# Every fourth weight rest made by ScalarE and an accumulating DMA in a float32 encoder trunk

## The chip, the core and the metric

The kernel runs on one core of a Trainium2 chip. The metric is the device time of one execution in microseconds (us); a kernel's time is the median of several runs. The five engines of a core (TensorE or PE, VectorE or DVE, ScalarE or ACT, GpSimd or POOL, SyncE or SP) run their own instruction queues in order and wait for each other by semaphores. DMAs are issued from such a queue (here from SP, POOL and twice from ACT) and are carried out by 16 DMA engines.

## The reference

A trunk of two layers on x of 256 tokens by 2048 features, float32. Per layer:

```
h = rms_norm(x);  z = h @ w_in                       # 2048 -> 11264 columns
ya = diff_attention(...); yb = dilated_mixture(...); yc = pool_mixer(...)
merged = g0 * (ya @ w_proj_a) + g1 * (yb @ w_proj_b) + g2 * (yc @ w_proj_c)
x = x + merged @ w_out
u = relu(rms_norm(x) @ w_up);  x = x + (u * u) @ w_down     # 2048 -> 8192 -> 2048
```

and a last rms_norm. Nearly all of the work is matmuls of the 256 tokens with weights that are read from HBM once.

## The kernel before, in words

To hold float32 accuracy at the rate of the type fp32r, each operand is split into a main part hi (the value rounded to fp32r) and a rest lo (value minus hi), and a product is three matmuls: hi with hi, hi with lo, lo with hi. `split` does that for activations, `convert` for weights.

The weights come in **steps** of 256 rows by 512 columns (512 KB). `add_unit` (L138) lists them; a unit is one block of 512 output columns, which is eight steps of a 2048-row weight (two or three of the projections' weights). There are 992 steps: per layer 80 for the inputs of the branches, 96 for the gates with 32 of the projections between them, 32 for w_out and 256 for the MLP, where four quarters of four w_up units are each followed by four w_down units.

`run_steps` (L180) goes through the steps. In step i it issues, in four slots, the step's matmuls, and in slot 2 (L201 to L203) the conversion of step i+3 and the load of the step four after the last one converted:

```
if slot == CONVERT_SLOT:
    convert(min(i + AHEAD, 2 * i + 1))
    fetch(st["cv"] - 1 + RAW_BUFS)
```

`fetch` (L143) loads a step into a tile raw by a DMA on SP's queue (L147); there are RAW_BUFS = 4 raw buffers. `convert` (L151) makes whi on ScalarE (L157) and wlo on VectorE (L158); there are AHEAD + 1 = 4 buffers of each. Buffers go around in order, so step j uses buffer j mod 4, and a buffer is free when its last reader is done: of raw the subtraction of wlo, of whi and wlo the matmuls. `by_token` (L162; activation stationary, 12 matmuls of 512 columns per step) is used by all units but w_up's, which go by `by_feature` (L172; weights stationary, 8 matmuls of 512 and 8 of 256 columns). After the last step of a unit its `after` function empties PSUM: `after_up` (L591) with ScalarE copies (u, L600), VectorE additions and squares (L601, L603) and, in the next two steps, splits into U (L242, L243); `after_down` (L613) with VectorE additions into x alone.

Other work is cut into pieces by generators, `side_work` (L115), and slipped between the slots: transposes, the attention (`attn_a`, `attn_b`), the pooling. On POOL's queue stand their loads of bias tables (`load_bias`, L364: biasa of 128 KB, biasb of 384 KB), the loads of the pooling bands (L488), the last norm's weight final_g (L631), the additions into merged (L538) and the small powers of the norms.

The order on each engine is the order in which this program issues; nothing reorders it later.

Of the kernel before, what the change touches and what calls it, by code (L numbers as in the profile page):

```python
# [10 lines left out]
F32 = mybir.dt.float32  # L11
FR = mybir.dt.float32r
BF16 = mybir.dt.bfloat16
ACTF = mybir.ActivationFunctionType
ALU = mybir.AluOpType
# [21 lines left out]
AHEAD = 3  # L37
CONVERT_SLOT = 2
RAW_BUFS = 4


def shape_constants():
    """Arrays that depend on the shapes alone: identity, T5 buckets of all
    distances, the windows of the dilated groups, the pooling bands."""
    ident = np.eye(128, dtype=np.float32)
    rel = (S - 1) - np.arange(512)
    half, exact = REL_BUCKETS // 2, REL_BUCKETS // 4
    n = np.abs(rel)
    nf = np.maximum(n, 1).astype(np.float32)
    ratio = (np.log(nf / np.float32(exact)) / np.float32(math.log(REL_MAX / exact))).astype(np.float32)  # L50
    large = exact + (ratio * np.float32(half - exact)).astype(np.int32)
    large = np.minimum(large, half - 1)
    bucket = np.where(rel > 0, half, 0) + np.where(n < exact, n, large)
    onehot = (np.arange(REL_BUCKETS)[:, None] == bucket[None, :]).astype(np.float32)
    window = np.zeros((REL_HEADS, 512), np.float32)
    for g, r in enumerate(DILATION):
        reach = (128, 512, 2048)[g] // (2 * r) * r
        ok = (rel % r == 0) & (n <= reach)
        window[A_HEADS + 4 * g:A_HEADS + 4 * g + 4, :] = np.where(ok, 0.0, NEG_INF)[None, :]
    pos = np.arange(S)  # L60
    band = np.zeros((S, len(C_WINDOWS), S), np.float32)
    for g, win in enumerate(C_WINDOWS):
        rad = win // 2
        lo, hi = np.clip(pos - rad, 0, S), np.clip(pos + rad + 1, 0, S)
        inside = (pos[:, None] >= lo[None, :]) & (pos[:, None] < hi[None, :])
        band[:, g, :] = inside / (hi - lo).astype(np.float32)[None, :] - np.eye(S)
    return {"c_ident": ident, "c_onehot": onehot, "c_window": window, "c_band": band.astype(np.float32)}
# [3 lines left out]
def encoder_trunk(ctx: ExitStack, tc: tile.TileContext, I, out: bass.AP):  # L71
    nc = tc.nc
# [28 lines left out]
    def tr_tile(shape, name):  # L101
        return ps_t.tile(shape, F32, tag="tr", name=name)

    # ---------------------------------------------------------------- side work
    lanes = []
    queue = []
    N_LANES = 2
# [5 lines left out]
        lanes.append([gen, False])  # L113

    def side_work():  # L115
        """The next piece of every side task, one at a time."""
        wait[0] -= 1
        if queue and busy[0] < N_LANES and wait[0] <= 0:
            lanes.append([queue.pop(0)(), True])
            busy[0] += 1  # L120
            wait[0] = SPACING
        for lane in list(lanes):
            yield lane
# [6 lines left out]
            if lane[1]:  # L130
                busy[0] -= 1

    # ---------------------------------------------------------------- weights
    steps = []
    st = {"dma": 0, "cv": 0}
    raw_t, hl_t = {}, {}
# [14 lines left out]
    def convert(upto):  # L151
        while st["cv"] <= min(upto, len(steps) - 1):
            j = st["cv"]
            r = raw_t.pop(j)
            hi = hl_p.tile([128, 2, BLK], FR, tag="hi", name="whi")
            lo = hl_p.tile([128, 2, BLK], FR, tag="lo", name="wlo")
            nc.scalar.activation(out=hi, in_=r, func=ACTF.Copy)  # L157
            nc.vector.tensor_tensor(out=lo, in0=r, in1=hi.bitcast(F32), op=ALU.subtract)  # L158
            hl_t[j] = (hi, lo)
            st["cv"] += 1  # L160

    def by_token(ps, a, kc, n, w, kk, t):  # L162
        """ps[token tile t] += act[kc].T @ W, the activation stationary."""
        hi, lo = w
        ts = slice(128 * t, 128 * t + 128)
        first, last = kc == 0, kc == n - 1
        o = ps[t][:, 0, :] if isinstance(ps, list) else ps[:, t, :]
        nc.tensor.matmul(o, a[:, kc, 0, ts], hi[:, kk, :], start=first, stop=False)  # L168
        nc.tensor.matmul(o, a[:, kc, 0, ts], lo[:, kk, :], start=False, stop=False)  # L169
        nc.tensor.matmul(o, a[:, kc, 1, ts], hi[:, kk, :], start=False, stop=last)  # L170

    def by_feature(ps, a, kc, n, w, kk, j):  # L172
        """ps[j] = [main | rest] of W[:, feature tile j].T @ act[kc], the weights stationary."""
        hi, lo = w
        fs = slice(128 * j, 128 * j + 128)
        first, last = kc == 0, kc == n - 1
        nc.tensor.matmul(ps[j], hi[:, kk, fs], a[:, kc, :, :], start=first, stop=False)  # L177
        nc.tensor.matmul(ps[j][:, S:2 * S], lo[:, kk, fs], a[:, kc, 0, :], start=False, stop=last)  # L178
# [41 lines left out]
                    u["after"](ps)  # L220

    def feature_banks(u):
        """Four PSUM banks; every other unit borrows those of the attention and the transposes."""
        if L["c"]["up"] % 2 == 0:
            g = [ps_g.tile([128, 2, BLK], F32, tag="g", name="acc") for _ in range(2)]
            u["groups"] = [(g[0], 0, 2), (g[1], 2, 2)]
            banks = [g[0][:, 0, :], g[0][:, 1, :], g[1][:, 0, :], g[1][:, 1, :]]
        else:
            a = ps_s.tile([128, 2, BLK], F32, tag="sc", name="acc")
            b = [ps_t.tile([128, 1, BLK], F32, tag="tr", name="acc") for _ in range(2)]  # L230
            u["groups"] = [(a, 0, 2), (b[0], 2, 1), (b[1], 3, 1)]
            banks = [a[:, 0, :], a[:, 1, :], b[0][:, 0, :], b[1][:, 0, :]]
        L["c"]["up"] += 1
        L["groups"] = u["groups"]
        return banks

    # ---------------------------------------------------------------- pieces
    def split(dst, src, scale=None):
        """dst[:, 0] gets the leading bits of src (times scale), dst[:, 1] the rest."""
        hi, lo = dst  # L240
        if scale is None:
            nc.scalar.activation(out=hi, in_=src, func=ACTF.Copy)  # L242
# [4 lines left out]
                                           op0=ALU.mult, op1=ALU.subtract)  # L247

    class Norm:
        """Statistics of the rows of x, block by block, and x * g transposed."""  # L250

        def __init__(self, g):
            self.ss = sm_p.tile([128, 2, NB], F32, tag="ss", name="ss", bufs=2)
# [30 lines left out]
        nc.scalar.activation(out=junk, in_=src, func=ACTF.Square, accum_out=dst)  # L284

    def rsqrt_mean(ss, n, name, w=2):
        """(mean + eps) ** -0.5 from partial sums of squares."""
        ms = sm_p.tile([128, w], F32, tag="ms", name="ms")
        rs = sm_p.tile([128, w], F32, tag=name, name=name, bufs=3)
        nc.vector.tensor_reduce(out=ms, in_=ss, axis=AX.X, op=ALU.add)  # L290
# [6 lines left out]

    L = {}

    # ---------------------------------------------------------------- q, k, v  # L300
    def qkv_tile():
        c = L["c"]
        if "Q" not in c:
# [173 lines left out]
            split((yT[:, h, 0, ts], yT[:, h, 1, ts]), tr, gsub[:, l:l + 1])  # L477
        return gen

    # ---------------------------------------------------------------- pooling  # L480
    def after_c(ps):
        c = L["c"]
        l = c["l"]
# [29 lines left out]
                yield  # L513
        start(task())

    # ---------------------------------------------------------------- gates
    def after_gate(ps):
        c = L["c"]
        g = one.tile([128, 2, BLK], F32, tag="gate", name="gate")
# [36 lines left out]
                start(task())  # L556
        return f

    # ---------------------------------------------------------------- residual
    def add_x(ps, n, scale=None, tiles=(0, 1)):  # L560
        cols = slice(n * BLK, (n + 1) * BLK)
        for t in tiles:
# [96 lines left out]
        c["rs8"] = sm_p.tile([128, 2], F32, tag="rs8", name="rs8", bufs=2)  # L659
        nc.vector.tensor_scalar(out=c["rs8"], in0=c["norm"].rs, scalar1=HD ** -0.5, scalar2=None, op0=ALU.mult)  # L660

    # ---------------------------------------------------------------- set-up
    def setup_norm1():
        tr = tr_tile([128, 16 * DEPTH], "v1t")
        nc.tensor.transpose(tr, vin1, ident[0:16 * DEPTH, 0:16 * DEPTH])
# [62 lines left out]
        nc.tensor.matmul(tr, ones, dl, start=True, stop=True)  # L728
        nc.vector.tensor_copy(out=neglam, in_=tr)

    # ---------------------------------------------------------------- program
    def queue_attention(kind):
        def add():
            c = L["c"]
# [102 lines left out]
```

## Time and profile before

| | |
|---|---|
| median of 3 runs | 2905.48 us (2901.34 to 2905.69) |
| span of the profiled execution, first to last instruction | 2904.1 us |
| PE busy | 2884.4 us, 99% |
| VectorE busy | 1582.5 us, 54% |
| ScalarE busy | 1353.5 us, 47% |
| GpSimd busy | 110.2 us, 4% |
| mean granted TensorE clock | 0.998 |
| mean busy share of the DMA engines | 0.63, 186 GB/s |

The profile is one execution. Its own time is given by its span alone; it is 1.4 us under the median of the runs. DMA instructions on an engine's queue are not counted as busy time of that engine. A PE that is busy 99% issues matmuls nearly all the time; matmuls overlap, so their durations add up to more than the time they take (a matmul of 512 columns lasts 0.39 us, and the next starts sooner).

### The profile page before, as it was taken

Reading aid. Unit: us, or ns where it says so; the run is one execution under the profiler, and the core shown is the slowest. Engines: PE = TensorE matmul, PEld = TensorE weight load, DVE = VectorE, ACT = ScalarE, POOL = GpSimd, SP = SyncE. Lnnn points to the kernel's source line nnn. Section 1 sums busy time; section 2 is a strip of 40 time slices with the busy share of each in tenths; the row PEclk is TensorE's granted clock in tenths of the full one; section 3 lists DMA queues with packets and bytes.
Section 4 is the critical chain, followed back from the end, with each engine's and each line's share of the span. In section 5 each row is a group of like instructions: output and inputs, shape, how many; then the busy total and the mean of one; then the engine's idle time right before and its main releaser. Section 6 shows DMA issues by size and latency. Waiting matters only on the chain.

```text
span 2904.1 us, 35814 instructions
## 1 busy us (share of the span) xinstructions
PE 2884.4 (99%) x13942; PEld 2396.0 (83%) x13942; DVE 1582.5 (54%) x1901; ACT 1353.5 (47%) x1716; POOL 110.2 (4%) x128
## 2 busy tenths in 40 slices
PE   8999999999999999999999999999999999999998
PEld 7877888888888888888888778888888888888887
DVE  5456544555655655555544565445555555555564
ACT  5455545444543434444444554544444444344443
POOL 1000001000000000000000000011100000000001
PEclk9999999999999999999999999999999999999999
DMA  7656766665666666666576567666656566666664
GB/s 236 193 159 177 196 173 158 188 188 182 186 195 192 181 197 188 190 184 192 188 206 186 161 176 200 168 165 192 183 187 200 190 189 188 193 179 198 190 188 156
DMA packets 275994, 540.00 MB, mean 186 GB/s; under 512 B 17044, under 2 KB 17230, under 8 KB 275696
## 3 DMA queue, kind: packets, MB, share of 16 engines
q1 hardware_dynamic: 271344, 523.63, 59.4%
q0 software_dynamic: 4144, 13.28, 3.0%
q8 instruction: 109, 1.79, 0.2%
q10 hardware_dynamic: 336, 0.80, 0.1%
q14 instruction: 61, 0.50, 0.0%
HBM read 535.51 MB, written 2.13 MB: 185 GB/s over the span
## 4 chain that ended last, share of the span: by engine, by line
PE 97%; DMA 1%; DVE 1%; issue 0%; ACT 0%; POOL 0%; POOLq 0%; DVEq 0%; SPq 0%; ACTq 0%
PE acc L168 23%; PE acc L170 23%; PE acc L169 22%; PE acc L177 16%; PE acc L178 8%; PE scb L385 1%; PE ob L412 1%; DMA biasb<-bias_d 1%; PE sca L435 1%; DMA raw<-in_w_in_dram 0%; PE xt L274 0%; PE oa L462 0%; PE qkt L344 0%; PE etb L402 0%; DVE wlo L158 0%
## 5 line engine op out<-in xcount | busy, mean ns | idle before, releaser
L158 DVE TENSOR_TENSOR wlo<-raw,whi 128x1024 fp32r<-128x1024 f32 x992 | 1225.4, 1238 | 1045.6 <-ACT whi L157 1037.5
L157 ACT ACTIVATE whi<-raw 128x1024 fp32r<-128x1024 f32 x992 | 1045.9, 1057 | 1049.5 <-PE acc L170 673.0
L177 PE MATMUL acc<-H,whi 128*128 128x512 f32 x2048 | 723.9, 399 | 0.6
L178 PE MATMUL acc<-H,wlo 128*128 128x256 f32 x2048 | 574.2, 280 | 0.0
L168 PE MATMUL acc<-whi,H 128*128 128x512 f32 x1408 | 569.8, 405 | 0.0
L170 PE MATMUL acc<-whi,H 128*128 128x512 f32 x1408 | 551.0, 391 | 0.0
L169 PE MATMUL acc<-wlo,H 128*128 128x512 f32 x1408 | 550.0, 391 | 0.5 <-DVE wlo L158 0.5
L177 PEld LDWEIGHTS acc<-H,whi 128*128 128x128 f32 x2048 | 384.7, 188 | 97.8 <-DVE x L567 2.5
L168 PE MATMUL acc<-whi,U 128*128 128x512 f32 x1024 | 399.1, 390 | 0.0
L170 PE MATMUL acc<-whi,U 128*128 128x512 f32 x1024 | 398.5, 389 | 0.0
L169 PE MATMUL acc<-wlo,U 128*128 128x512 f32 x1024 | 398.4, 389 | 0.0
L178 PEld LDWEIGHTS acc<-H,wlo 128*128 128x128 f32 x2048 | 386.6, 189 | 0.3
L168 PEld LDWEIGHTS acc<-whi,H 128*128 128x128 f32 x1408 | 265.2, 188 | 63.1 <-issue 11.5
L170 PEld LDWEIGHTS acc<-whi,H 128*128 128x128 f32 x1408 | 264.9, 188 | 57.6
L169 PEld LDWEIGHTS acc<-wlo,H 128*128 128x128 f32 x1408 | 265.7, 189 | 52.2 <-DVE wlo L158 2.1
L170 PEld LDWEIGHTS acc<-whi,U 128*128 128x128 f32 x1024 | 192.2, 188 | 40.4
L168 PEld LDWEIGHTS acc<-whi,U 128*128 128x128 f32 x1024 | 192.2, 188 | 39.7
L169 PEld LDWEIGHTS acc<-wlo,U 128*128 128x128 f32 x1024 | 192.3, 188 | 39.5
L168 PE MATMUL acc<-whi,M 128*128 128x512 f32 x256 | 101.2, 395 | 0.0
L170 PE MATMUL acc<-whi,M 128*128 128x512 f32 x256 | 99.9, 390 | 0.0
L169 PE MATMUL acc<-wlo,M 128*128 128x512 f32 x256 | 99.6, 389 | 0.0
L538 POOL TENSOR_TENSOR merged<-merged,gp 128x512 f32<-128x512 f32 x32 | 50.5, 1598 | 575.8 <-DVE gp L537 575.8
(153 smaller groups left out, 1709.3 us busy)
## 6 DMA issues: line engine op xcount, KB each, us to landing
raw<-in_w_in_dram SPq DMA_DIRECT2D x352, 512.0 KB, 4.1
raw<-in_w_up_dram SPq DMA_DIRECT2D x256, 512.0 KB, 3.8
raw<-in_w_down_dram SPq DMA_DIRECT2D x256, 512.0 KB, 4.5
raw<-in_w_out_dram SPq DMA_DIRECT2D x64, 512.0 KB, 4.3
raw<-in_w_proj_a_dram SPq DMA_DIRECT2D x24, 512.0 KB, 7.5
raw<-in_w_proj_b_dram SPq DMA_DIRECT2D x24, 512.0 KB, 4.2
raw<-in_w_proj_c_dram SPq DMA_DIRECT2D x16, 512.0 KB, 4.6
biasb<-bias_d POOLq DMA_DIRECT2D x16, 384.0 KB, 9.4
```

The lines of the kernel that those rows point to most:

```text
L157: nc.scalar.activation(out=hi, in_=r, func=ACTF.Copy)
L158: nc.vector.tensor_tensor(out=lo, in0=r, in1=hi.bitcast(F32), op=ALU.subtract)
L168: nc.tensor.matmul(o, a[:, kc, 0, ts], hi[:, kk, :], start=first, stop=False)
L169: nc.tensor.matmul(o, a[:, kc, 0, ts], lo[:, kk, :], start=False, stop=False)
L170: nc.tensor.matmul(o, a[:, kc, 1, ts], hi[:, kk, :], start=False, stop=last)
L177: nc.tensor.matmul(ps[j], hi[:, kk, fs], a[:, kc, :, :], start=first, stop=False)
L178: nc.tensor.matmul(ps[j][:, S:2 * S], lo[:, kk, fs], a[:, kc, 0, :], start=False, stop=last)
L385: nc.tensor.matmul(sc[:, g, :], head_rows(c, "qb", 4 * g + j)[:, ts], head_rows(c, "kb", 4 * g + j), start=True, stop=True)
L412: nc.tensor.matmul(o[:, g, :], eT[:, 2 * g + kc, :], c["vb"][:, kc, col:col + 64], start=kc == 0, stop=kc == 1)
L435: nc.tensor.matmul(sc[:, 2 * i, :], c["qa"][r, h, ts], c["ka"][r, h, :], start=True, stop=True)
L538: nc.gpsimd.tensor_tensor(out=mg[:, t, cols], in0=mg[:, t, cols], in1=e, op=ALU.add)
```

## The change

In steps 3, 7, 11 and so on, a quarter of all, ScalarE writes the negated weights, rounded to fp32r, into wlo (that is minus whi), and a DMA issued from POOL's queue adds the raw weights to it. The VectorE subtraction of these steps is gone. Docstrings and comment lines go too, which moves line numbers by five: whi is L158 now, the negated copy L160, the accumulating DMA L161 and the subtraction of the other steps L163.

```diff
 AHEAD = 3
 CONVERT_SLOT = 2
 RAW_BUFS = 4
+BY_DMA = 4
...
             nc.scalar.activation(out=hi, in_=r, func=ACTF.Copy)
-            nc.vector.tensor_tensor(out=lo, in0=r, in1=hi.bitcast(F32), op=ALU.subtract)
+            if j % BY_DMA == BY_DMA - 1:
+                nc.scalar.activation(out=lo, in_=r, func=ACTF.Copy, scale=-1.0)
+                nc.gpsimd.dma_start(out=lo, in_=r, accum_op=ALU.add)
+            else:
+                nc.vector.tensor_tensor(out=lo, in0=r, in1=hi.bitcast(F32), op=ALU.subtract)
             hl_t[j] = (hi, lo)
```

On SP the loads stay in their order. Here the end of a w_up unit's loads and the first of w_down's are shown, before and then changed; in brackets are the semaphores a load waits for (DVE: VectorE's, DMAHW: of DMAs issued by SP, DMASW: of DMAs issued by POOL):

```order
L147 DMA raw<-in_w_up_dram 128x2x512 [waits DMAHW5_49,DVE_49]
L147 DMA raw<-in_w_up_dram 128x2x512 [waits DMAHW6_49,DVE_49]
L147 DMA raw<-in_w_up_dram 128x2x512 [waits DMAHW7_49,DVE_49]
L147 DMA raw<-in_w_up_dram 128x2x512 [waits DMAHW0_49,DVE_49]
L147 DMA raw<-in_w_up_dram 128x2x512 [waits DMAHW1_49,DVE_49]
L147 DMA raw<-in_w_down_dram 128x2x512 [waits DMAHW2_49,DVE_49]
```

```order
L148 DMA raw<-in_w_up_dram 128x2x512 [waits DMAHW6_49,DVE_49]
L148 DMA raw<-in_w_up_dram 128x2x512 [waits DMAHW5_49,DMASW2_49]
L148 DMA raw<-in_w_up_dram 128x2x512 [waits DMAHW7_49,DVE_49]
L148 DMA raw<-in_w_up_dram 128x2x512 [waits DMAHW0_49,DVE_49]
L148 DMA raw<-in_w_up_dram 128x2x512 [waits DMAHW2_49,DVE_49]
L148 DMA raw<-in_w_down_dram 128x2x512 [waits DMAHW1_49,DMASW3_49]
```

Every fourth load now waits for a DMA of POOL's queue in place of VectorE.

On ScalarE, at the border of two w_up units, the evacuations u and splits U of the unit that ended stand around the first whi of the next one; before, and then changed:

```order
L157 ACTIVATE whi<-raw 128x1024 [waits DMAHW0_49,DVE_49,PE_49]
L600 ACTIVATE u<-acc 128x512 [waits PE_49]
L600 ACTIVATE u<-acc 128x256 [waits PE_49] x2
L242 ACTIVATE U<-u 128x2x256 [waits DVE_49]
L157 ACTIVATE whi<-raw 128x1024 [waits DMAHW1_49,Activation_49]
L242 ACTIVATE U<-u 128x2x256 [waits DVE_49]
```

```order
L158 ACTIVATE whi<-raw 128x1024 [waits DMAHW0_49,DVE_49,PE_49]
L605 ACTIVATE u<-acc 128x512 [waits PE_49]
L605 ACTIVATE u<-acc 128x256 [waits PE_49] x2
L247 ACTIVATE U<-u 128x2x256 [waits DVE_49]
L158 ACTIVATE whi<-raw 128x1024 [waits DMAHW1_49,Activation_49]
L160 ACTIVATE wlo<-raw 128x1024 [waits DMASW0_49]
L247 ACTIVATE U<-u 128x2x256 [waits DVE_49]
```

The whi of position 3 of the next unit is a changed step's, and the negated copy follows it, ahead of the second split.

On POOL, in the stretch where the dilated attention loads its biases and the projections are added into merged; before, and then changed:

```order
L364 DMA biasb<-bias_d 128x3x256 [waits DMASW7_49]
L364 DMA biasb<-bias_d 128x3x256 [waits DMASW0_49]
L538 TENSOR_TENSOR merged<-merged,gp 128x512 [waits DVE_49] x2
L364 DMA biasb<-bias_d 128x3x256 [waits DMASW1_49]
L364 DMA biasb<-bias_d 128x3x256 [waits DMASW2_49]
```

```order
L369 DMA biasb<-bias_d 128x3x256 [waits DMASW0_49]
L161 DMA wlo<-raw 128x1024 [waits DMASW7_49,DMAHW5_49,PE_49,Activation_49]
L369 DMA biasb<-bias_d 128x3x256
L161 DMA wlo<-raw 128x1024 [waits DMASW1_49,DMAHW1_49,PE_49,Activation_49]
L543 TENSOR_TENSOR merged<-merged,gp 128x512 [waits DVE_49] x2
L369 DMA biasb<-bias_d 128x3x256 [waits DMASW0_49]
L161 DMA wlo<-raw 128x1024 [waits DMASW3_49,DMAHW5_49,PE_49,Activation_49]
```

The accumulating DMA, which waits for ScalarE's negated copy, stands between the bias loads and additions that were neighbours.

## Rows read from the trace of the kernel before

**Rows 1.** The page: busy time of TensorE, and the chain that ended last, by engine.

```profile
PE 2884.4 (99%) x13942; PEld 2396.0 (83%) x13942; DVE 1582.5 (54%) x1901; ACT 1353.5 (47%) x1716; POOL 110.2 (4%) x128
...
PE 97%; DMA 1%; DVE 1%; issue 0%; ACT 0%; POOL 0%; POOLq 0%; DVEq 0%; SPq 0%; ACTq 0%
```

**Rows 2.** Who waited for whom, TensorE alone: us in total, times, longest.

```profile
PE ob L412 <- DVE eTb L406: 2.3, 2, 1.3
PE acc L169 <- DVE wlo L158: 0.5, 2, 0.3
```

**Rows 3.** Timeline, end of a w_up unit: start, us, instruction, [idle before <-releaser].

```profile
828.05 1.06 ACT L157 ACTIVATE whi<-raw 128x1024 fp32r<-128x1024 f32 x1 [1.71 <-PE acc L177]
830.82 1.06 ACT L157 ACTIVATE whi<-raw 128x1024 fp32r<-128x1024 f32 x1 [1.71 <-PE acc L177]
832.33 0.60 ACT L600 ACTIVATE u<-acc 128x512 f32<-128x512 f32 x1 [0.44 <-PE acc L178]
...
835.73 1.05 ACT L157 ACTIVATE whi<-raw 128x1024 fp32r<-128x1024 f32 x1
...
836.80 1.22 DVE L158 TENSOR_TENSOR wlo<-raw,whi 128x1024 fp32r<-128x1024 f32 x1 [0.26 <-ACT whi L157]
```

**Rows 4.** Timeline, ScalarE, in the w_down unit after it.

```profile
844.62 1.06 ACT L157 ACTIVATE whi<-raw 128x1024 fp32r<-128x1024 f32 x1 [1.61 <-PE acc L170]
847.34 1.06 ACT L157 ACTIVATE whi<-raw 128x1024 fp32r<-128x1024 f32 x1 [1.66 <-PE acc L170]
```

**Rows 5.** Stretches, whi alone: its length, busy us (count), clock, DMA share, GB/s.

```profile
65.00:639.30 574.30, 195.28 (x187) 1.00 0.64 180
639.30:743.40 104.10, 38.77 (x37) 1.00 0.59 186
743.40:1457.40 714.00, 270.44 (x256) 1.00 0.62 189
```

**Rows 6.** The page's costliest groups: wlo and whi (busy, mean ns, idle before).

```profile
L158 DVE TENSOR_TENSOR wlo<-raw,whi 128x1024 fp32r<-128x1024 f32 x992 | 1225.4, 1238 | 1045.6 <-ACT whi L157 1037.5
L157 ACT ACTIVATE whi<-raw 128x1024 fp32r<-128x1024 f32 x992 | 1045.9, 1057 | 1049.5 <-PE acc L170 673.0
```

**Rows 7.** Who waited for whom, SP's queue: us in total, times, longest.

```profile
SPq L147 <- DVE wlo L158: 2107.9, 906, 6.4
```

**Rows 8.** DMAs to landing: issues (median us), and lines L147 and L488.

```profile
raw<-in_w_up_dram SPq DMA_DIRECT2D x256, 512.0 KB, 3.8
raw<-in_w_down_dram SPq DMA_DIRECT2D x256, 512.0 KB, 4.5
...
biasb<-bias_d POOLq DMA_DIRECT2D x16, 384.0 KB, 9.4
biasa<-bias_d POOLq DMA_DIRECT2D x24, 128.0 KB, 3.5
...
final_g<-in_final_g_dram POOLq DMA_DIRECT2D x1, 1024.0 KB, 5.2
...
DMA to landing us min/median/max: 3.4/4.3/15.2
...
DMA to landing us min/median/max: 6.8/8.7/10.5
```

**Rows 9.** The page's DMA queues: packets, MB, share of 16 engines.

```profile
q1 hardware_dynamic: 271344, 523.63, 59.4%
q0 software_dynamic: 4144, 13.28, 3.0%
```

**Rows 10.** Timeline of TensorE near 425 us, and the stretch after the gap.

```profile
425.28 0.72 PE L412 MATMUL ob<-qkv,eTb 128*128 128x64 f32 x4 [1.28 <-DVE eTb L406]
...
426.33 0.63 PE L169 MATMUL acc<-wlo,H 128*128 128x512 f32 x1
426.75 0.63 PE L170 MATMUL acc<-whi,H 128*128 128x512 f32 x1
...
425.70:429.10 3.40, 3.40 (x11) 2.72 (x10) 1.95 (x3) 1.68 (x4) 0.06 (x1) 0.51 0.82 193
```

## The prediction

> **What bounds the kernel now.** I read the engine shares and the chain of waits first: TensorE is busy 99% of the span and its matmuls are 97% of the chain that ended last [rows 1]. The list of who waited for whom, cut to TensorE, then shows how little is lost to anything the change could relieve: 2.3 us behind a VectorE copy in the attention and 0.5 us behind wlo, in the whole run [rows 2]. VectorE, which the change relieves, is not on the path. What matters is therefore whether the new way of making lo is ready in time.
>
> For that I read the beat. Where matmuls run alone, ScalarE's whi instructions start 2.77 us apart in an up unit and 2.72 us apart in a down unit [rows 3, 4]; each waits for TensorE to give back a buffer. So four weight steps, one turn of the change, last 11.1 us (up) or 10.9 us (down). The two matmul sub-layers together have 2 x 256 steps; one of them takes 714.0 us [rows 5], so one up unit of eight steps has 22.2 us and one down unit 21.8 us. The 32 steps of w_out take 104.1 us, 13.0 us per four. In the stretch ahead of it 187 steps take 574.3 us, 12.3 us per four, because attention and transposes are mixed in, unevenly [rows 5].
>
> **Parts that cost or give next to nothing.** 248 VectorE subtractions of 1.238 us go [rows 6]: 307 us off an engine that is busy 54%. Even if every wait of rows 2 went with them, that is 2.8 us, 0.1% of the time. 248 more ScalarE instructions come, of the shape, types and function of whi, so 1.057 us each [rows 6]: 262 us more, 47% becomes 56% of the span; they run in ScalarE's idle time before the next buffer (1.7 us in each plain step [rows 3]). If that cover were gone, each would delay the next whi by its 1.06 us, and a whi is made some three steps before its use.
>
> **The part that counts: a longer ring.** RAW_BUFS is 4, and so is the turn of the change, so the changed steps always use the same raw buffer. SP can load step j+4 into it only when nobody reads step j there. Today the reader is done with the subtraction, and SP's loads wait for it 906 times [rows 7]. Changed, SP waits for the accumulating DMA to land, and the next three loads stand behind that wait. So a turn can't be shorter than this chain: raw load to landing, whi, the negated copy, the accumulating DMA from issue to landing, and around again.
>
> Terms: the load 3.8 us, the median of w_up (all loads: least 3.4, median 4.3) [rows 8]; I take the low median because SP has just been held back, so that little is in flight beside the first load. Two ScalarE instructions, 2.1 us [rows 6]. Handoffs 0.15 us: the whi of 835.73 ends at 836.78, and VectorE, which waits for it, starts at 836.80 [rows 3]; I count four such, with some reserve for the two DMAs among them. That is 6.05 us without the accumulation.
>
> The accumulation itself, 512 KB within SBUF, reads two operands and writes one. No row shows such a DMA. From below: 128 KB through POOL's queue land in 3.5 us (biasa). From above: 384 KB in small rows in 9.4 us (biasb) [rows 8]. Nearest by the bytes read, two times 512 KB, are the 1 MB loads on POOL's queue: final_g in 5.2 us, the pooling bands in 6.8 and, in the crowded start, 10.5 us [rows 8]. I take 5.6 us, nearer to final_g, which like the accumulation is issued alone in the middle of the run. The turn is then 6.05 + 5.6 = 11.65, say 11.7 us; the ends are 9.6 us (3.5) and 15.5 us (9.4).
>
> That two operands are read weighs most in this choice. The Trainium skill says the same of reductions in a DMA (Collectives: The Full Stack, section on the bandwidth ceiling): the add costs nothing, but two sources have to be read, and the rate is halved. No run here shows that yet; by it 1 MB is the size to price, as the sum already does, and a price per byte written would give about the raw load's 3.8 us instead.
>
> Against the beat: in a down unit two turns take 23.4 instead of 21.8 us, +1.6 us, 32 times: 51 us. In an up unit something is added: the changed step at position 3 is converted while step 0 runs, and whi stands on ScalarE behind the evacuations (u) and the first split (U) of the unit before. There whi starts at 835.73, 4.91 us after the one before instead of 2.77 [rows 3]. Of that I add 2.3 us to the ring, because a raw load that lands 3.8 us after the turn begins would wait from there to about 6.1 us (2.7 us of the last step, then 3.4 us from 832.33 to 835.73). So an up unit takes 2 x 11.7 + 2.3 = 25.7 instead of 22.2 us, 32 times 3.5: 112 us. w_out, 13.0 us per turn, hides it. In the other 104 turns (992 steps without 512 and 64, over four) the mean of 12.3 is above 11.7, but the plain half of them is at 10.9: 52 x 0.8 = 42 us. There POOL's in-order queue also holds the accumulation behind biasb loads and the merged additions; 10 us for that. Sum: 51 + 112 + 42 + 10 = 215 us.
>
> The sum stands against the profiled span, 2904.1 us; the median of the runs is 1.4 us more, and I add that: 2905.5 + 215 = 3120 us. Two executions of this kernel agree within some 0.2% (2901 to 2906), so that I count as no change.
>
> The DMA engines can carry it: 248 x 0.524 MB are 130 MB. The load queue takes 59.4% for 523.63 MB, POOL's queue 3.0% for 13.28 MB [rows 9]: 15% more at the first rate, 29% at the second, on 63%. At the upper end transfers would queue, which is one more reason for a wide range upwards.
>
> **Rivals.**
>
> Hidden (the other side). If the accumulation lands like one raw load of its size, 3.8 us [rows 8], the turn is 9.9 us: below 10.9, and in an up unit 2 x 9.9 + 2.3 = 22.1 against 22.2. Everything is covered, 2906 us. It decides at 3.9 us for up units and at 4.8 us for down units. For it: the DMA engines are free 37% of the time, and the whole add happens in SBUF. Against it: 128 KB already take 3.5 us on this queue, and no 1 MB load lands under 5.2 us [rows 8]. The Trainium skill's fit for a DMA that GpSimd issues (DMA: Bandwidth & Descriptors, section on the anatomy of one DMA) is 2.0 us plus the bytes at 436 GB/s; as an estimate that is 3.2 us for 512 KB and 4.4 us for 1 MB, and by 3.2 us the change would be hidden, at 2906 us, and by 4.4 us up units alone would lose 1.0 us each, 2937 us. The trace disagrees upwards: 5.2 us or more for 1 MB.
>
> Slow accumulation. If the read, add and write-back go at the pace of biasb, 9.4 us, the turn is 15.5 us: up 32 x 11.1, down 32 x 9.2, w_out 16 x 2.5, the others 104 x 3.2, together 1022 us, 3930 us. At 7.5 us the turn is 13.6: 234 + 173 + 10 + 135 = 552, 3458 us. For it: POOL's queue took long for 384 KB; against it: those were 1 KB rows from HBM, these are 4 KB rows in SBUF.
>
> The clock falls. At 425.28 TensorE had been idle for 1.28 us; in the 3.4 us that follow the granted clock is 0.51, the 1.2 GHz level, and matmuls start 0.42 us apart instead of 2.72/12 = 0.23 [rows 4, 10]. That costs about 1.6 us (8 matmuls in 3.4 us, which else take 1.8). The stalls forecast here are of that size. If each of 248 turns lost 1.6 us, 397 us more, 3517 us; where the ring is the bound TensorE has that time to spare, so I take half, 3320 us.
>
> Faster: only by rows 2, 0.1%, or by effects on the loads that nothing here shows.
>
> **How the numbers follow.** Forecast (accumulation between 4.2 and 7.5 us) 0.57; hidden 0.12; slow, over 7.5 us, 0.15; clock 0.13; faster 0.03. Slower by over 0.2% holds the forecast, slow and clock: 0.85; same 0.12; faster 0.03. At 4.2 us the turn is 10.25: only up units lose, 32 x 0.6 = 19 us, 2925; at 7.5 us 3458. The range is 2925 to 3470 us; it takes in the clock rival's middle and leaves out most of hidden and slow.
>
> **What would show it.** Right: TensorE waits for wlo's DMA once per turn, mostly in MLP stretches; SP waits in its queue for that DMA; the landing time of wlo's DMA is near 5.6 us and whi of changed steps start 11.7 us apart or more; up units lose about twice what down units lose; VectorE falls to some 1276 us busy, ScalarE rises to 1616. Wrong: TensorE still 99% busy (hidden); landings over 7.5 us (slow); half clock in many slices (clock); or TensorE waiting for whi of unchanged steps, which would mean that the loads behind SP's wait, not the ring, set the time.

## The result and the profile after

The changed kernel takes 2976.33 us in the median (2974.36 to 2978.6) where the kernel before takes 2904.22 us (2901.34 to 2905.69) beside it: a ratio of 1.0249, 95% interval 1.0237 to 1.0262. It is slower, as forecast, by 72 us and not by 215. The profiled execution spans 2972.6 us, 68.5 more than that of before, and the sums by stage below go by this difference.

The page of the changed kernel: engines, queues, the costliest groups that the change touches, and DMAs with their median time to landing.

```profile
PE 2900.4 (98%) x13942; PEld 2391.0 (80%) x13942; DVE 1284.9 (43%) x1653; ACT 1581.4 (53%) x1964; POOL 321.0 (11%) x376
...
q1 hardware_dynamic: 271344, 523.63, 51.3%
q0 software_dynamic: 39856, 143.32, 27.4%
...
L158 ACT ACTIVATE whi<-raw 128x1024 fp32r<-128x1024 f32 x992 | 1043.6, 1056 | 934.8 <-PE acc L175 580.5
L163 DVE TENSOR_TENSOR wlo<-raw,whi 128x1024 fp32r<-128x1024 f32 x744 | 915.6, 1237 | 1193.3 <-ACT whi L158 1180.0
...
L160 ACT ACTIVATE wlo<-raw 128x1024 fp32r<-128x1024 f32 x248 | 259.0, 1044 | 0.0
...
raw<-in_w_up_dram SPq DMA_DIRECT2D x256, 512.0 KB, 4.6
raw<-in_w_down_dram SPq DMA_DIRECT2D x256, 512.0 KB, 5.1
wlo<-raw POOLq DMA_DIRECT2D x248, 512.0 KB, 4.8
```

Beside [rows 1, 6, 8, 9]: VectorE and ScalarE moved as the instruction counts say (1582.5 to 1284.9 us, 1353.5 to 1581.4 us; ScalarE by 228 us and not by 262, because the copy starts 0.96 us after a whi that lasts 1.06), the accumulation lands in 4.8 us, and the loads became slower (up 3.8 to 4.6 us, down 4.5 to 5.1 us).

Who waited for whom, changed kernel, TensorE and SP's queue: us in total, times, longest. These answer to [rows 2, 7].

```profile
PE acc L174 <- DMA wlo<-raw: 27.0, 32, 2.7
PE acc L183 <- DMA wlo<-raw: 22.4, 25, 1.1
...
PEld acc L174 <- DMA wlo<-raw: 48.5, 55, 3.0
PEld acc L183 <- DMA wlo<-raw: 30.3, 25, 1.4
...
SPq L148 <- DVE wlo L163: 1298.4, 534, 7.4
SPq L148 <- DMA wlo<-raw: 768.9, 245, 11.4
```

TensorE's matmuls now wait 49.4 us for wlo's DMA, in 57 waits where there are 248 turns; its weight loads (PEld), which overlap with the matmuls before them, wait 78.8 us in 80. The busy time of PE is also 16.0 us longer (2884.4 to 2900.4 us), which was not taken apart. L183 is the by_feature matmul of the w_up units: 25 waits of at most 1.1 us, near one per up unit.

The timeline shows one. First ScalarE and POOL at the border of two up units, then TensorE (start, us, instruction, idle before):

```profile
775.00 1.06 ACT L158 ACTIVATE whi<-raw 128x1024 fp32r<-128x1024 f32 x1 [1.77 <-PE acc L182]
776.59 0.60 ACT L605 ACTIVATE u<-acc 128x512 f32<-128x512 f32 x1 [0.53 <-PE acc L183]
778.00 0.60 ACT L605 ACTIVATE u<-acc 128x512 f32<-128x512 f32 x1 [0.81 <-PE acc L183]
779.95 0.64 ACT L247 ACTIVATE U<-u 128x512 fp32r<-128x512 f32 x1 [1.35 <-DVE u L608]
780.49 1.04 ACT L158 ACTIVATE whi<-raw 128x1024 fp32r<-128x1024 f32 x1
781.44 1.04 ACT L160 ACTIVATE wlo<-raw 128x1024 fp32r<-128x1024 f32 x1
...
782.77 0.86 POOL L161 DMA_DIRECT2D wlo<-raw  x1 [12.45 <-ACT wlo L160]
...
787.61 0.39 PE L183 MATMUL acc<-H,wlo 128*128 128x256 f32 x1 [0.99 <-DMA wlo<-raw]
```

The changed whi starts 5.49 us after the one before it in place of 2.77, because u and U are ahead of it [rows 3]. From its start to the first matmul that reads wlo are 7.12 us: 1.99 for whi and the copy, 0.29 to POOL's issue, the rest the accumulation (782.77 to 787.56, a landing of 4.79 us) and 0.05 to the matmul, which comes 0.99 us late. With whi at its beat wlo would have been there 1.7 us early.

A down unit of the changed kernel, ScalarE, which answers to [rows 4]:

```profile
904.75 1.06 ACT L158 ACTIVATE whi<-raw 128x1024 fp32r<-128x1024 f32 x1 [1.71 <-PE acc L175]
905.71 1.04 ACT L160 ACTIVATE wlo<-raw 128x1024 fp32r<-128x1024 f32 x1
907.42 1.06 ACT L158 ACTIVATE whi<-raw 128x1024 fp32r<-128x1024 f32 x1 [0.66 <-PE acc L175]
910.14 1.06 ACT L158 ACTIVATE whi<-raw 128x1024 fp32r<-128x1024 f32 x1 [1.66 <-PE acc L175]
912.86 1.06 ACT L158 ACTIVATE whi<-raw 128x1024 fp32r<-128x1024 f32 x1 [1.66 <-PE acc L175]
915.63 1.06 ACT L158 ACTIVATE whi<-raw 128x1024 fp32r<-128x1024 f32 x1 [1.71 <-PE acc L175]
```

From one changed step to the next are 10.88 us, the beat of before; nothing waits for a load in these rows. The ring of 11.7 us is not there.

Where the 68.5 us lie, from the starts of the first evacuation of each unit in both timelines: the 24 intervals from one up unit to the next grew by 24.2 us in all, the 8 from an up to a down unit by 9.9, those that begin with a down unit by 13.0 (most stay at 21.76; the growth is in the last quarter of each layer), the stretch ahead of the first up unit by 10.8 and the stretch between the two layers' MLPs by 10.7.

### The profile page after: what moved, and what is told of

Same layout as the page of the kernel before. It is cut to its first block, busy times and chain, and to the rows that moved or that the text cites. A ratio compares the mean times of both kernels' runs of the same rounds, so it can differ in the third digit from the quotient of the medians.

```text
span 2972.6 us, 36292 instructions
## 1 busy us (share of the span) xinstructions
PE 2900.4 (98%) x13942; PEld 2391.0 (80%) x13942; DVE 1284.9 (43%) x1653; ACT 1581.4 (53%) x1964; POOL 321.0 (11%) x376
## 5 line engine op out<-in xcount | busy, mean ns | idle before, releaser
L158 ACT ACTIVATE whi<-raw 128x1024 fp32r<-128x1024 f32 x992 | 1043.6, 1056 | 934.8 <-PE acc L175 580.5
L163 DVE TENSOR_TENSOR wlo<-raw,whi 128x1024 fp32r<-128x1024 f32 x744 | 915.6, 1237 | 1193.3 <-ACT whi L158 1180.0
L183 PE MATMUL acc<-H,wlo 128*128 128x256 f32 x2048 | 576.9, 282 | 22.4 <-DMA wlo<-raw 22.4
L161 POOL DMA_DIRECT2D wlo<-raw x248 | 214.3, 864 | 2378.3 <-ACT wlo L160 2177.7
L183 PEld LDWEIGHTS acc<-H,wlo 128*128 128x128 f32 x2048 | 386.8, 189 | 30.7 <-DMA wlo<-raw 30.3
L160 ACT ACTIVATE wlo<-raw 128x1024 fp32r<-128x1024 f32 x248 | 259.0, 1044 | 0.0
L173 PE MATMUL acc<-whi,M 128*128 128x512 f32 x256 | 101.3, 396 | 0.0
```

The source lines that it names most:

```text
L160: nc.scalar.activation(out=lo, in_=r, func=ACTF.Copy, scale=-1.0)
L161: nc.gpsimd.dma_start(out=lo, in_=r, accum_op=ALU.add)
```

## The experiments

Two theories stand against each other. **Lateness (A):** the accumulation itself comes too late for TensorE, because whi and the copy stand behind u and U on ScalarE and 7.1 us follow. **The ring**, as predicted: SP can't reload the buffer before the accumulation has landed, and raw weights come late. The expectations call the ring C, and name others, such as the DMAs' traffic as such (D), where they stand. The runs are told by question, not by date. To make room in the core's memory, those with a fifth buffer or an extra tile keep three small set-up tiles in the gate's buffer.

| run | edit | median us | ratio to before, interval |
|---|---|---|---|
| the change | | 2976.33 | 1.0249, 1.0237 to 1.0262 |
| e3_neg_dve | VectorE adds, no DMA | 2904.2 | 1.0005, 0.9995 to 1.0016 |
| e7_dummy | same DMA, result unread | 2911.57 | 1.0028, 1.0013 to 1.0043 |
| e11_copy | e7 with a plain copy | 2898.91 | 0.9982, 0.9971 to 0.9994 |
| e5_neg_first | copy and DMA ahead of whi | 2939.05 | 1.0126, 1.0109 to 1.0143 |
| e4_turn1 | steps 1, 5, 9 ... | 2957.46 | 1.0194, 1.0176 to 1.0212 |
| e6_both | e5 and e4 | 2950.62 | 1.0167, 1.0152 to 1.0182 |
| e12_halves | e5, two DMAs of 256 KB | 2942.96 | 1.0129, 1.0111 to 1.0147 |
| e2_raw5 | five raw buffers | 2968.75 | 1.0233, 1.0213 to 1.0253 |
| e10_neg_raw5 | e5 and e2 | 2947.79 | 1.0148, 1.0131 to 1.0166 |
| e8_fixed_ring | step j in raw buffer j mod 4 | 3028.27 | 1.0436, 1.0416 to 1.0456 |
| e13_swap | e5, two loads exchanged | 3061.95 | 1.054, 1.0521 to 1.056 |
| e14_early | copy and DMA a step earlier | 2963.28 | 1.0212, 1.0195 to 1.0228 |
| e15_early_swap | e13 and e14 | 3119.02 | 1.0748, 1.0731 to 1.0765 |
| e16_map | raw buffers by a written rule | 2970.28 | 1.0232, 1.0217 to 1.0246 |
| e17_neg_map | e5 and e16 | 2922.49 | 1.0067, 1.0055 to 1.0079 |
| e9_half | every second step | 3306.45 | 1.1402, 1.1364 to 1.144 |

### Is it the DMA, and is it its traffic or its lateness?

**e3_neg_dve** keeps ScalarE's copy and lets VectorE add the raw weights.

```diff
-                nc.gpsimd.dma_start(out=lo, in_=r, accum_op=ALU.add)
+                nc.vector.tensor_tensor(out=lo, in0=r, in1=lo.bitcast(F32), op=ALU.add)
```

> The changed steps keep ScalarE's negated copy, but VectorE adds the raw weights to it in place of the DMA. Theory A (lo comes too late: whi, negated copy and DMA take 7.1 us from the free buffer, and whatever stands ahead of whi on ScalarE comes on top; TensorE has about 8.3 us): the chain falls to 2.0 + 1.25 = 3.3 us, all waits of TensorE for lo go, time 2900 to 2912 us (ratio 0.998 to 1.003). Theory B (ScalarE's additional 259 us are what costs): loss stays, about 2976 us. Theory C (the raw buffers are held too long by the DMA, so loads come late): also back to about 2905 us, so this run separates A and C from B only.

Measured: 2904.2 us, no difference to before. ScalarE's extra instructions cost nothing, although it is as busy as in the changed kernel (1580.8 us); all of the loss hangs on the DMA.

**e7_dummy** makes every lo by the subtraction and adds raw by DMA into a tile that nobody reads. **e11_copy** copies raw there.

```diff
-                nc.scalar.activation(out=lo, in_=r, func=ACTF.Copy, scale=-1.0)
-                nc.gpsimd.dma_start(out=lo, in_=r, accum_op=ALU.add)
-            else:
-                nc.vector.tensor_tensor(out=lo, in0=r, in1=hi.bitcast(F32), op=ALU.subtract)
+                nc.gpsimd.dma_start(out=scratch, in_=r, accum_op=ALU.add)   # e11: without accum_op
+            nc.vector.tensor_tensor(out=lo, in0=r, in1=hi.bitcast(F32), op=ALU.subtract)
```

> All steps are subtracted by VectorE as before the change; in steps 3, 7, ... a DMA of the same kind and size adds the raw weights to a scratch tile that nobody reads, so the traffic, POOL's work and the hold on the raw buffer are there and no matmul waits for it. Theory A: 2902 to 2914 us (ratio up to 1.004). Theory D (traffic as such delays weight loads or slows VectorE): a good part of the 72 us, 2930 to 2976 us.

> As the run with the scratch tile, but a plain copy of the raw weights in place of the accumulation: same bytes written, one operand read. If the second operand is what the accumulation pays for, POOL's queue takes some 14% of the DMA engines in place of 26%, and a landing 4 to 5 us in place of 6.2; the time goes to 2900 to 2910 us. If the write-back or the software queue sets the price, both stay near 26% and 6 us.

Measured: 2911.57 and 2898.91 us. The traffic, SP's waits for the DMA included, costs 8 us of the 72; the other 64 come only when the result is waited for. e7 is not lighter on the raw buffers than the change: in 243 of 247 turns the load of the next changed step waits for the accumulation (SP waits 1724.0 us in all, against 768.9), and still that costs no more, because nobody reads the result. The pages' DMA queues and issues, e7 and then e11:

```profile
q0 software_dynamic: 39856, 143.32, 26.3%
...
scratch<-raw POOLq DMA_DIRECT2D x248, 512.0 KB, 6.2
```

```profile
q0 software_dynamic: 39856, 143.32, 16.2%
...
scratch<-raw POOLq DMA_DIRECT2D x248, 512.0 KB, 5.6
```

Both write the same bytes. Without the 3.0% that the queue had before [rows 9], the accumulations take 23.3% of the engines' time and the copies 13.2%, a factor of 1.77: an accumulation costs the engines nearly two transfers. The prediction priced it by the two operands that it reads, and in engine time this pair bears that out. The Trainium skill (Collectives: The Full Stack, section on the bandwidth ceiling) has a reduce at half the rate of a copy because of the two reads; the factor of 1.77 is near that. The landing time grows much less, from 5.6 to 6.2 us in the median.

### Is it ScalarE's queue?

**e5_neg_first** issues the negated copy and its DMA ahead of whi, **e4_turn1** changes steps 1, 5, 9 in place of 3, 7, 11, away from the border of the units, and **e6_both** does both.

```diff
+            if j % BY_DMA == BY_DMA - 1:          # e4, e6: == 1
+                nc.scalar.activation(out=lo, in_=r, func=ACTF.Copy, scale=-1.0)
+                nc.gpsimd.dma_start(out=lo, in_=r, accum_op=ALU.add)
             nc.scalar.activation(out=hi, in_=r, func=ACTF.Copy)      # e4: stays ahead, as in the change
```

> In changed steps the negated copy and the DMA are issued ahead of whi, so the DMA starts one ScalarE instruction (1.04 us) sooner after the same wait; nothing else differs. Theory A (lo comes too late by 0.5 to 1.2 us in up units): up units lose 0.0 to 0.3 us each in place of 1.0; the loss of 72 us falls to 15 to 40 us, 2918 to 2942 us. Theory D (traffic as such): 2976 us, unchanged.

> The changed steps are 1, 5, 9, ... in place of 3, 7, 11, ...: in an up unit their whi is no longer queued behind the evacuation and the first split of the unit before. Theory A: the 32 x 1.0 us of up units go, and the last unit's 4 us as well; 2925 to 2945 us. Theory C (raw buffers held too long): the turn is as long as before, about 2976 us. Theory D (DMA traffic as such slows loads): 2976 us.

> Changed steps 1, 5, 9, ... and the negated copy ahead of whi. Theory A: in the MLP nothing is left to lose; outside it the 37 us that steps 1, 5, 9 lost fall by a half to two thirds; 2912 to 2930 us. Theory D: about 2957 us, as with the moved steps alone.

Measured: e5 2939.05 us, half of the loss. The intervals between up units grew by 1.0 us in all, in place of 24.2: a copy that ends 0.94 us earlier after u is nearly the 0.99 us that TensorE had waited. So the up units' share is lateness behind ScalarE's queue. In e4 (2957.46 us) the intervals between up units grew by 9.1 us in place of 24.2, but its two stretches outside the MLPs grew by 21.3 and 15.4 us in place of 10.8 and 10.7. The longest wait of TensorE there, 4.8 us, is for the accumulation of step 1, at the very start of the run; the rest was not taken apart. e4 and e6 (2950.62 us) both miss what was expected of them; e6 should have been the best and is worse than e5, and its intervals between up units grew by 15.9 us.

ScalarE's waits for raw weights show what comes up instead, in e5 and then in e6 (us in total, times, longest):

```profile
ACT wlo L159 <- DMA raw<-in_w_down_dram: 161.6, 47, 4.8
ACT wlo L159 <- DMA raw<-in_w_up_dram: 114.8, 36, 4.2
```

```profile
ACT wlo L159 <- DMA raw<-in_w_down_dram: 183.1, 58, 4.9
ACT wlo L159 <- DMA raw<-in_w_up_dram: 125.0, 48, 4.6
```

In the changed kernel, where whi comes first, whi's waits for the same loads are 11.8 and 6.8 us. With the copy first, the changed steps' loads are late: the ring that the changed kernel in most turns doesn't have.

**e12_halves** is e5 with the DMA in two halves, to start the first matmuls on the first half.

```diff
-                nc.gpsimd.dma_start(out=lo, in_=r, accum_op=ALU.add)
+                for kk in range(2):
+                    nc.gpsimd.dma_start(out=lo[:, kk, :], in_=r[:, kk, :], accum_op=ALU.add)
```

> Negated copy ahead of whi, and the accumulation in two DMAs of 256 KB, one for each 128 rows of the step; matmuls that use the second half wait for it alone, which in by_token is 1.4 us later than the first, and in by_feature 0.7 us. Traffic and ScalarE's work are those of the run with the copy first. If what is left there (37 us) is lateness of single accumulations that share the DMA engines with loads, the first half lands some 1 us sooner and the second has slack: 2912 to 2930 us. If POOL's second issue (0.86 us) and the fixed part of a landing eat that up, 2935 to 2950 us.

Measured: 2942.96 us. Half the bytes land in 4.4 us (two halves fly together) where e5's whole lands in 5.0, so there is little to win, and POOL issues twice as often.

### Where the ring went

**e2_raw5** gives the changed kernel a fifth raw buffer, **e10_neg_raw5** gives one to e5.

```diff
-RAW_BUFS = 4
+RAW_BUFS = 5
```

> A fifth raw buffer (room made by placing the small set-up tiles of the lambdas in the gate's buffer), the change as it is. Theory A: no difference, 2968 to 2980 us, up units still 1.0 us longer than before the change. Theory C: SP no longer waits for the accumulation in time to matter, back to 2905 to 2925 us.

> Negated copy and DMA ahead of whi, and a fifth raw buffer. With the copy first alone 37 us were left, and in most of the steps where TensorE still waited, ScalarE had started 0.1 us after a raw load landed. If that is a second limit, the raw buffers (C), which only shows once the first is gone, the fifth buffer takes most of it: 2906 to 2922 us. If what is left comes from slow accumulations (5.5 to 6.5 us beside the loads) the time stays at 2930 to 2945 us.

Measured: 2968.75 us, a loss of 2.33% in place of 2.49%, with intervals that overlap: raw buffers hardly bind the changed kernel. In e10, 2947.79 us, the waits of e5 for raw are gone and the time is no better; the accumulations land in 5.7 us there (5.0 in e5). Why five buffers do worse than the four of e17 below was not settled.

**e8_fixed_ring** ties step j to raw buffer j mod 4, as the prediction assumed it of the changed kernel.

```diff
-            t = raw_p.tile([128, 2, BLK], F32, tag="raw", name="raw")
+            t = raw_p.tile([128, 2, BLK], F32, tag=f"raw{j % RAW_BUFS}", name="raw", bufs=1)
```

> The raw buffers are four single ones, step j in buffer j mod 4, so that the load of step j+4 always waits for the accumulation of step j, as the prediction had assumed (in the change 203 of 247 such loads go to another buffer). By the measured parts the turn would be 3.9 (load) + 2.0 + 0.3 + 4.8 + 0.1 = 11.1 us against a beat of 10.9 (down) and 11.3 (up, two turns per unit of 22.6): with the ring as bound, down units lose 0.4 us each more than now, up units about 2 us more, 3040 to 3070 us. If lateness at ScalarE alone counts (A), 2970 to 2985 us.

Measured: 3028.27 us, between the two times expected and nearer to the ring's. ScalarE in down units of e8, and SP's queue:

```profile
901.83 1.06 ACT L158 ACTIVATE whi<-raw 128x1024 fp32r<-128x1024 f32 x1 [4.17 <-DMA raw<-in_w_down_dram]
...
913.40 1.06 ACT L158 ACTIVATE whi<-raw 128x1024 fp32r<-128x1024 f32 x1 [3.95 <-DMA raw<-in_w_down_dram]
...
925.70 1.06 ACT L158 ACTIVATE whi<-raw 128x1024 fp32r<-128x1024 f32 x1 [4.71 <-DMA raw<-in_w_down_dram]
...
937.25 1.06 ACT L158 ACTIVATE whi<-raw 128x1024 fp32r<-128x1024 f32 x1 [3.67 <-DMA raw<-in_w_down_dram]
```

```profile
SPq L148 <- DMA wlo<-raw: 2190.3, 247, 11.8
SPq L148 <- DVE wlo L163: 254.9, 253, 4.1
```

Here it is: turns of 11.57, 12.30 and 11.55 us, each begun by a load that SP could issue only after the accumulation. The chain that ended last runs around the ring in these units, and its pieces are the ring's terms (start us, us, what):

```profile
897.41 4.32 DMA raw<-in_w_down_dram
...
901.83 1.06 ACT whi L158
902.89 0.95 ACT wlo L160
903.85 0.28 issue
904.13 4.77 DMA wlo<-raw
...
908.96 4.34 DMA raw<-in_w_down_dram
```

So what does the changed kernel do with its buffers? The rows of the two programs tell. SP's loads carry tile numbers here; 9862 is a changed step's and 9880 that of the step behind it. The changed kernel, and then e8:

```
L148 DMA raw_9862<-in_w_up_dram 128x2x512 [waits DMAHW6_49,DVE_49]
L148 DMA raw_9880<-in_w_up_dram 128x2x512 [waits DMAHW5_49,DMASW4_49]
```

```
L148 DMA raw_9862<-in_w_up_dram 128x2x512 [waits DMAHW5_49,DMASW4_49,Activation_49]
L148 DMA raw_9880<-in_w_up_dram 128x2x512 [waits DMAHW6_49,DVE_49]
```

In the changed kernel the changed step's load waits for a VectorE subtraction, and it is the next step's load that waits for the accumulation. The builder gave the two buffers the other way around, in 203 of 247 turns: a buffer that an accumulation has held next goes to a plain step, and in these turns no changed step waits for the one before it. In the kernel before, all loads go around in order. In e5 and e12 the assignment is the fixed order in 220 turns (in e10 too, where five buffers in order give the held one to a plain step), in e6 in 208, in e7 and e11 in 243, in e8 and e14 in all 247. So an edit that only moves the copy ahead of whi, as e5 does, closes the ring. What the builder goes by was not looked into.

**e13_swap** (e5, with a changed step's load issued one place later), **e14_early** (copy and DMA right behind the whi of the step before, with five wlo buffers) and **e15_early_swap** were made before this was understood.

```diff
+            if j % BY_DMA == BY_DMA - 1 and 3 < j < len(steps) - 1:    # e13, e15
+                continue
+            for i in ([j, j - 1] if j % BY_DMA == 0 and j > 4 else [j]):
+                nc.sync.dma_start(out=raw_t[i], in_=steps[i][2].rearrange("(k p) f -> p k f", p=128))
...
+            negate(j + 1)       # e14, e15: in convert(j), behind its whi
```

> The negated copy and its DMA stand ahead of whi, as in e5_neg_first (2939 us), and the program now puts the load that waits for the accumulation one place later on SP's queue, behind the next step's load. Theory S (what was left in e5, 35 us, is SP's wait: loads that stand behind it come late, and ScalarE waits for raw): 2908 to 2925 us, and ScalarE's waits for raw of w_down (161.6 us in 47 waits in e5) fall below 40 us. Rival R (what was left is the accumulation itself, landing in 5 to 8 us beside the loads): 2930 to 2945 us with the waits for raw gone all the same.

> The negated copy and its DMA are issued one step earlier (right behind the whi of the step before), with five wlo buffers; SP's loads stand in order. Theory R (lateness alone): the accumulation has a step, 2.7 us, more, so 2908 to 2920 us, near e7_dummy's 2911.6 us, which carries the same traffic and waits for nothing. Theory S (SP's wait delays the loads): 2930 to 2950 us, no better than e5_neg_first, with ScalarE waiting over 150 us for raw.

> Both: one step earlier, and the waiting load one place later on SP. If lateness and SP's order are all there is, 2905 to 2915 us, with TensorE's waits for wlo's DMA below 10 us in all. If something else costs the rest (the accumulations' traffic slowing the loads beyond what e7_dummy showed), over 2920 us.

Measured: 3061.95, 2963.28 and 3119.02 us; no theory had such times. In e13 and e15 the edit did the reverse of what was meant. The builder again gave the held buffer to the next step (in 196 and 246 turns), whose load the edit put ahead: now the changed step's load, free to go, stood behind it. ScalarE's copies in e13 start by the ring:

```profile
901.72 1.06 ACT L162 ACTIVATE wlo<-raw 128x1024 fp32r<-128x1024 f32 x1 [7.51 <-DMA raw<-in_w_down_dram]
...
913.07 1.06 ACT L162 ACTIVATE wlo<-raw 128x1024 fp32r<-128x1024 f32 x1 [5.76 <-DMA raw<-in_w_down_dram]
...
924.72 1.06 ACT L162 ACTIVATE wlo<-raw 128x1024 fp32r<-128x1024 f32 x1 [5.07 <-DMA raw<-in_w_down_dram]
```

Turns of 11.35 and 11.65 us, although whi is no longer part of the chain. In e14 the ring is closed in all turns, and ScalarE waits 421.6 us for raw of w_down, w_up and w_in: a step of more time for the accumulation is worth nothing while the load is late.

**e16_map** writes the changed kernel's assignment into all turns, and **e17_neg_map** does the same in e5. `ring` holds the buffers, the newest first.

```diff
+            if j % BY_DMA == BY_DMA - 1 and j > BY_DMA:
+                ring[2:] = [ring[3], ring[2]]
+            b = ring.pop() if j >= RAW_BUFS else j
+            ring.insert(0, b)
-            t = raw_p.tile([128, 2, BLK], F32, tag="raw", name="raw")
+            t = raw_p.tile([128, 2, BLK], F32, tag=f"raw{b}", name="raw", bufs=1)
```

> The changed kernel with the raw buffers handed out by a rule in all turns: a changed step takes the buffer of the step three before it, which VectorE frees, and the step behind it takes the one that the accumulation holds, as the changed kernel has it in 203 of 247 turns. If that assignment is why the changed kernel escapes the ring, and e8_fixed_ring (step j in buffer j mod 4, 3028 us) does not: 2965 to 2980 us, like the changed kernel's 2976. If e8's loss came from its fixed tags in another way: 3010 us or more.

> The negated copy and its DMA ahead of whi, as in e5_neg_first (2939 us, where 220 of 247 turns have the ring closed), with the assignment of e16_map. Theory S (what was left in e5 is the closed ring): 2905 to 2922 us, and ScalarE's waits for raw of w_down and w_up, 276 us in e5, below 40 us. Theory R (what was left is the accumulation, which lands later where more loads fly beside it): 2930 to 2950 us with those waits gone and wlo's DMA landing in 5.5 us or more, as in e10_neg_raw5.

Measured: e16 2970.28 us, as expected if the assignment alone parts the changed kernel from e8, by 58 us with the same tags and the same instructions; and e17 2922.49 us, half a microsecond above what theory S said and 7.5 below R. The waits of e17:

```profile
ACT wlo L164 <- DMA raw<-in_w_down_dram: 8.7, 5, 1.8
...
PE acc L179 <- DMA wlo<-raw: 7.2, 9, 3.2
```

ScalarE's copies wait 8.7 us for raw of w_down and not at all for that of w_up (161.6 and 114.8 us in e5), though the accumulation lands in 5.4 us (5.0 in e5), so R's landing nearly came true and its time did not. The 72 us now part in three. The turns in which the changed kernel's ring is closed cost up to 6 (2976.33 to 2970.28 us, and the intervals of the two ratios overlap). The place of the copy behind whi, with the assignment held the same, costs 48 (2970.28 to 2922.49 us). The 18 that stay hold the traffic, 8 by e7; in the profile they lie mostly ahead of the first up unit and between the MLPs (5.3 and 6.7 us) and were not taken apart.

### Twice the turns

**e9_half** changes every second step.

```diff
-BY_DMA = 4
+BY_DMA = 2
```

> Every second step by the DMA (496 accumulations). The DMA engines' busy share would be 51% for the loads and 2 x 27%, over 100% at the present speed, so the engines become a second limit: theory A alone would give about twice the loss, 3030 to 3060 us; with the engines full 3080 to 3250 us, landings of the accumulation well over 5 us, and waits in all units, down units too.

Measured: 3306.45 us, above all that was expected. The page, and TensorE's waits:

```profile
PE 3015.1 (91%) x13942; PEld 2427.5 (73%) x13942; DVE 981.7 (30%) x1405; ACT 1814.5 (55%) x2212; POOL 532.7 (16%) x624
...
q1 hardware_dynamic: 271344, 523.63, 46.3%
q0 software_dynamic: 75568, 273.35, 45.5%
...
wlo<-raw POOLq DMA_DIRECT2D x496, 512.0 KB, 6.2
```

```profile
PE acc L174 <- DMA wlo<-raw: 230.6, 166, 5.9
```

Twice the accumulations cost 402 us in place of 72. The two queues take 92% of the DMA engines' time, and the accumulation lands in 6.2 us in place of 4.8. The mean granted clock of this execution is 0.978 (0.998 before), so a part of the loss may be TensorE's clock behind its waits; how much falls to clock, queues and ring was not taken apart.

No version with the accumulation beats the kernel before; the nearest, e17, stays 0.67% behind.

## Why the prediction was right and wrong

**Direction and the place of the wait: right.** TensorE waits for wlo's DMA, at the up units above all (34 us there with the borders to down units, 13 in down units), behind the evacuations u and splits U that the prediction named [rows 3]; but in 57 waits and not once per turn. VectorE's relief shows nowhere: TensorE's wait for VectorE's copy in the attention was 2.3 us [rows 2] and is 3.7 now; no run gives the relief alone. The clock did not fall: the mean granted clock is 0.999 (0.997 to 0.999 over the four executions).

**The step that failed: "the changed steps always use the same raw buffer", so that the turn is a ring of 11.7 us against a beat of 10.9.** The premise, "step j uses buffer j mod 4", was read from the kernel before, where it holds, and carried over. The changed program doesn't do it in 203 of 247 turns, and turns in most down units are 10.88 us. The sign stood in the rows of SP after the change that were on record with the prediction: the last of them, the load of the first w_down step, waits for DMASW3, and position 0 is not a changed step; the row above it, the load of position 7, which is a changed step, waits for VectorE. It was read as "every fourth load waits for a DMA of POOL's queue", and which one was not asked. Where the premise is made true, in e8, the ring is there, near the size that was worked out: turns of 11.55 to 12.30 us in the rows shown, and 41 us lost in down units where 51 were forecast; the whole loss there is 124 us, not 215.

**Up units: 3.5 us each forecast, about 1.0 measured, and by another way.** The 2.3 us delay on ScalarE was right in kind (whi starts 5.49 us after the one before it), but it was added to the ring. In the changed kernel it uses up the reserve that the accumulation has, and 1 us is left over. In e8, where there is a ring, the up units lose 46 us (30.3 and 15.8) and not 112: two turns of 11.7 us against 22.2 alone give 32 x 1.2 = 38, so the delay adds little there too, which fits a load that lands after the delay has passed.

**Terms.** Accumulation: 5.6 us taken, 4.8 measured (4.5 in the median of e8); the row of final_g was too far above. Loads: 3.8 us taken. All loads together became slower (4.6 and 5.1 us; 5.6 and 5.8 in e8), but the ring's term is the changed step's own load, 4.3 us in the chain of e8. So taking the low median had the right reason and was half a microsecond short. Handoffs: 0.15 us taken for all; from ScalarE to POOL's issue alone there are 0.28. In the ring's sum these errors nearly cancel, and that e8's turns come near 11.7 us is in part luck.

The same goes for the size of the whole. With the measured 4.8 us for the accumulation the prediction's own sum would have a turn of 10.85 us, 32 x 1.8 = 58 us in up units, nothing in down units and 10 for POOL: 68 us, close to the 72 measured, by a ring that the changed kernel mostly does not have. That hit would have been luck.

The 104 other turns and POOL's order: 52 us forecast; 21.5 us were lost outside the MLPs.

The Trainium skill's fit (DMA: Bandwidth & Descriptors, section on the anatomy of one DMA) gives, as an estimate, 3.2 us for 512 KB; in the trace of the changed kernel no accumulation landed under 4.5 us.

**SP's wait** was no cost in itself: 1724.0 us of waits for the DMA in e7, and 8 us of time. It costs where a changed step's load stands behind it and TensorE waits for what that step's accumulation makes (e8, e13, e15).

## What to carry to other kernels

Before a ring is priced, read from the changed program which load waits for which reader: an allocation may hand buffers around in another order than the code suggests, a small edit may change that order (e5), and here it alone was worth 58 us. A DMA in place of an engine's instruction is bound by its lateness: sum the time from the first free buffer to the first use, with the engine queue ahead of it, and put the instruction that starts the DMA first. And measure a DMA's traffic by itself, with its result unread.

## What was not expected of the hardware

An accumulating DMA of 512 KB within SBUF takes 1.77 times the engine time of a copy (23.3% against 13.2%), and its median landing differs by a tenth only (6.2 against 5.6 us). Half the bytes land in 4.4 us, beside their other half, where the whole lands in 5.0, so the landing time is far from going with the bytes. e11, which adds 248 useless copies, measures 0.9982 (0.9971 to 0.9994) of the time before. The interval leaves out 1, but 0.2% is also what two executions of one kernel differ by; no cause was looked for.
